# Placing every large SBUF tile of a decoder trunk at a multiple of 256 bytes

## The chip, the core and the metric

The kernel runs on one core of a Trainium2 chip. The metric is device time in microseconds (us), from runs of the whole kernel; lower is better. Engines are named as in the profile: PE is TensorE (PEld its weight loads), DVE is VectorE, ACT is ScalarE, POOL is GpSimd, SP is SyncE, whose queue (SPq) issues all the DMAs here.

## The reference

A decoder trunk of two layers on 1024 tokens of width 1024, 16 heads of 64. Each layer normalises, projects, mixes, gates and projects back:

```
h = rms_norm(x, norm_g[i])
if i % 2 == 0: o, gate = fox_mixer(h, ...)     # layer 1
else:          o, gate = dsw_mixer(h, cos, sin, ...)   # layer 2
x = x + (o * silu(gate)) @ w_out
```

The mixer of layer 1 ("fox") is causal attention over all earlier tokens with a forget bias: `s = q k / 8 + c_q - c_k`, softmax, times v, where `c` is a running sum of log-sigmoids and q and k are normalised per head. The mixer of layer 2 ("dsw") has three groups of queries, keys and values, with windows of 128 tokens at dilations 1, 4 and 16, rotary positions on the first 16 dimensions, and a softmax over the groups' log-sums that weighs their outputs.

## The kernel before

Matrices are held as pairs of fp16 numbers, a high part and the rest, so that each float32 product becomes three fp16 matmuls (`xh`·w high, `xh`·w low, `xl`·w high). A projection (L678, in `project`) takes one tile of 128 tokens against the 384 columns of a block of weights: 24 matmuls of 128 x 384, with a slice of `xh` or `xl` as the weights and the block's `w` as the moving operand. The output projections (L702, in `project_t`) do the reverse: `w` is loaded as weights and 512 columns of `xh` or `xl` move.

A block of weights goes through `raw` (loaded as float32, L605), a bound of its size (L615, L617), and the split into the fp16 pair `w` (L643, L644, or L646 to L648 on GpSimd). There are eight `raw` and eight `w` tiles of 3072 bytes a partition, two blocks' worth.

Attention runs by heads in pairs. `heads_tile` (L772 to L783) and `heads_pair` (L804 to L820) turn a projection into normalised queries and keys `hl`, a fp16 pair; a DMA transpose (L824) puts `hl` into `qk_t`, 12 blocks of 128 x 128. L844 makes the scores from `qk_t`, VectorE adds bias or mask and takes the minimum (L1091 in layer 1, L1319 in layer 2), ScalarE takes the exponential in place in `p` (L887; L1321, L1327) and casts it to the high half of `ph` (L890; L1331), GpSimd puts the rest into the low half (L893; L1332), and a second DMA transpose (L894; L1333) makes `ptt`, which is loaded as weights against the values `vt` (L901 to L903). In layer 2 the outputs of two groups go through HBM (`og` out, `cmb` back), are weighed on GpSimd (L1363, L1364), and are added to the third group's on VectorE (L1371).

The order of the work on every engine is set at the end by a planner (`order_engines`), which replays the recorded instructions with costs written into the program and fixes each engine's sequence. It knows tiles by name, shape and buffer count, and knows nothing of addresses.

SBUF tiles come from pools. `const`, `w`, `sb` and `sm` live through the kernel; a pool `layer` is opened for each layer, with a number of buffers for each tag. A pool puts its tiles one behind the other, each at the next multiple of 32 bytes of the partition. All pools are wrapped in the class `Listed`, which also notes each tile for the planner. Of the small tiles (statistics of 4 to 192 bytes a partition) there are many, and they shift what follows. Where the large tiles start, in bytes past a multiple of 256:

| tile | bytes a partition | before | after |
|---|---|---|---|
| `xh`, `xl` | 16384 | 128 | 0 |
| `raw`, `w`, `u`, `hl` | 2048 or 3072 | 96 | 0 |
| `p`, layer 1 / layer 2 | 512 to 4096 | 32 / 128 | 0 |
| `ph`, layer 1 / layer 2 | 1024 to 4096 | 32 / 224 | 0 |
| `ptt`, layer 1 / layer 2 | 1024 to 4096 | 32 / 224 | 0 |
| `qk_t` | 3072 | 128 | 0 |
| `vt` (three buffers) | 4128 | 32, 64, 96 | 0 |
| `og` (three buffers) | 1056 | 128, 160, 192 | 0 |
| `cmb` (four buffers) | 3168 | 224, 64, 160, 0 | 0 |

Of the kernel before, what the change touches and what calls it, by code (L numbers as in the profile page):

```python
# [84 lines left out]
            self.tick()  # L85


class Book:


# [16 lines left out]
class Listed:  # L107
# [2 lines left out]
        self.book, self.p, self.key, self.bufs, self.space = book, p, key, bufs, space  # L110

    def tile(self, shape, dtype, name, **kw):
        t = self.p.tile(shape, dtype, name=name, **kw)
        self.book.rows[t.tensor.name if hasattr(t, "tensor") else t.name] = (self.key + (kw.get("tag", name),), kw.get("bufs", self.bufs), self.space)
        return t
# [1419 lines left out]
```

## Time and profile before

| | us |
|---|---|
| median of 3 runs (lowest, highest) | 1687.83 (1684.5, 1690.51) |
| the profiled execution | 1688.37 |
| its span, first to last instruction | 1686.5 |
| idle time of PE in the span | 65.6 |

The page gives, for each engine, its busy time; the share of the chain that ended last ("PE pj L678 43%"); and, for groups of instructions, how often one ran, how long one took and what ended the idle time before it. Idle time of an engine that is not the bottleneck costs nothing. The DMA engines moved 292.84 MB in 662861 packets, 510208 of them under 512 bytes: the transposes move pieces of 256 bytes, 128 fp16 numbers.

The span has four parts: the start and the gates of layer 1 (to about 130 us), the attention of layer 1 (130 to 560), its output projection and the gates of layer 2 (560 to 740), and layer 2's attention (740 to 1640) with the last projection behind it.

### The profile page before, as it was taken

To read this page: it belongs to the slowest core of one execution; us is meant where nothing else is said; L and a number is where in the kernel's file an instruction comes from. 1 tells how busy PE (TensorE), PEld (TensorE's weight loads), DVE (VectorE), ACT (ScalarE), POOL (GpSimd) and SP (SyncE) were. 2 spreads that over 40 slices of the span, in tenths; PEclk is the share of its full clock that TensorE was granted. 3 is DMA by queue.
4 is the path that set the end of the run, shared out by engine and by line. 5 is a ranking of instruction groups with operands and counts; after the bars stand their busy time and mean duration, and the time that the engine had idled before them with its cause. 6 is when DMAs were issued, how large, how long until landed. Compare 5 with 4: busy or idle time off the path is not lost.

```text
span 1686.5 us, 37679 instructions
## 1 busy us (share of the span) xinstructions
PE 1620.9 (96%) x13342; PEld 1047.3 (62%) x13342; DVE 1184.2 (70%) x3663; ACT 1065.6 (63%) x2746; POOL 895.7 (53%) x1049
## 2 busy tenths in 40 slices
PE   6999999999988989999999999999999999999999
PEld 4666666666665436666666666666666666666644
DVE  7857677776777577567776787677776777767751
ACT  6656677676677456656666677566665666666630
POOL 5203566565545242145555566677686766757530
PEclk8999999999999999999999999999999999999999
DMA  7335999999999885347778798778787778878952
GB/s 250 110 122 127 199 213 205 203 185 207 213 195 215 230 264 174 126 91 150 148 150 164 158 214 186 151 151 191 170 165 151 151 174 160 186 150 170 218 157 100
DMA packets 662861, 292.84 MB, mean 174 GB/s; under 512 B 510208, under 2 KB 626944, under 8 KB 662672
## 3 DMA queue, kind: packets, MB, share of 16 engines
q1 hardware_dynamic: 662672, 290.44, 77.6%
q8 instruction: 104, 1.70, 0.4%
q14 instruction: 85, 0.70, 0.1%
HBM read 124.35 MB, written 41.22 MB: 98 GB/s over the span
## 4 chain that ended last, share of the span: by engine, by line
PE 57%; DMA 6%; DVE 6%; ACT 3%; issue 2%; SPq 1%; POOL 1%; DVEq 0%; ACTq 0%; POOLq 0%
PE pj L678 43%; PE pj L702 7%; PE s L844 4%; DMA ptt<-ph 3%; DMA qk_t<-hl 2%; DVE w L644 1%; PE ob L903 1%; PE ob L901 1%; PE ob L902 1%; DVE xs L1241 1%; SPq L894 1%; DMA yt<-y_d 1%; PE pt L712 0%; ACT w L643 0%; ACT ph L890 0%
## 5 line engine op out<-in xcount | busy, mean ns | idle before, releaser
L678 PE MATMUL pj<-w,xh 128*128 128x384 f16 (+2 forms) x4864 | 1174.9, 324 | 13.5 <-DVE w L644 5.9
L678 PE MATMUL pj<-w,xl 128*128 128x384 f16 (+2 forms) x2432 | 788.1, 324 | 5.5 <-DVE xl L1246 5.3
L678 PEld LDWEIGHTS <-xh 128*128 128x128 f16 x4864 | 466.8, 98 | 285.1 <-issue 7.2
L678 PEld LDWEIGHTS <-xl 128*128 128x128 f16 x2432 | 238.4, 98 | 163.5 <-issue 8.0
L893 POOL TENSOR_TENSOR ph<-p,ph 128x512 f16<-128x512 f32 (+3 forms) x176 | 172.7, 1003 | 154.0 <-issue 67.5
L819 POOL TENSOR_TENSOR hl<-u,hl 128x512 f16<-128x512 f32 x128 | 155.5, 1215 | 109.5 <-ACT hl L818 109.0
L1332 POOL TENSOR_TENSOR ph<-p,ph 128x768 f16<-128x768 f32 (+2 forms) x96 | 160.9, 1676 | 90.6 <-ACT ph L1331 80.0
L844 PE MATMUL s<-qk_t 128*128 128x128 f16 (+1 forms) x1504 | 163.7, 248 | 8.2 <-DMA qk_t<-hl 4.6
L702 PE MATMUL pj<-xh,w 128*128 128x512 f16 x512 | 158.2, 383 | 4.6 <-DVE xr L1471 2.9
L772 DVE TENSOR_TENSOR u<-pj,gr 128x256 f32<-128x256 f32 x256 | 107.5, 420 | 73.6 <-PE pj L678 72.2
L777 ACT ACTIVATE sq<-pj 128x256 f32<-128x256 f32 x256 | 96.5, 377 | 80.8 <-DVE u L772 80.1
L887 ACT ACTIVATE p<-p,acc 128x512 f32<-128x512 f32 (+2 forms) x192 | 111.4, 607 | 41.4 <-DVE acc L1091 39.9
L644 DVE SCALAR_TENSOR_TENSOR w<-raw,sws,w 128x768 f16<-128x768 f32 x96 | 127.0, 1324 | 10.2 <-ACT w L643 9.2
L844 PEld LDWEIGHTS <-qk_t 128*128 128x128 f16 x1504 | 115.5, 98 | 28.7 <-DMA qk_t<-hl 6.8
L702 PEld LDWEIGHTS <-w 128*128 128x128 f16 x768 | 74.5, 99 | 87.6 <-issue 8.4
L901 PEld LDWEIGHTS <-ptt 128*128 128x128 f16 x1136 | 106.0, 98 | 32.1 <-DMA ptt<-ph 21.9
L1321 ACT ACTIVATE p<-p,og 128x128 f32<-128x128 f32 (+1 forms) x256 | 104.2, 441 | 25.7 <-DVE og L1319 24.7
L615 ACT ACTIVATE jk<-raw 128x768 f16<-128x768 f32 (+2 forms) x88 | 72.2, 820 | 65.8 <-DMA raw<-in_w_dsw 38.1
L818 ACT CAST hl<-u 128x512 f16<-128x512 f32 x128 | 78.6, 614 | 55.0 <-DVE u L816 33.1
L783 DVE SCALAR_TENSOR_TENSOR vt<-pj,vt 128x128 f16<-128x128 f32 x256 | 73.5, 287 | 55.8 <-ACT vt L782 55.5
L902 PEld LDWEIGHTS <-ptt 128*128 128x128 f16 x1136 | 105.6, 97 | 10.0 <-issue 0.4
L903 PEld LDWEIGHTS <-ptt 128*128 128x128 f16 x1136 | 105.8, 97 | 0.5
(210 smaller groups left out, 2851.7 us busy)
## 6 DMA issues: line engine op xcount, KB each, us to landing
raw<-in_w_dsw SPq DMA_DIRECT2D x96, 384.0 KB, 4.0
raw<-in_w_fox SPq DMA_DIRECT2D x32, 384.0 KB, 4.0
og_d<-og SPq DMA_DIRECT2D x64, 132.0 KB, 3.0
cmb<-og_d SPq DMA_DIRECT2D x64, 132.0 KB, 2.8
bc<-c_d SPq DMA_DIRECT2D x32, 256.0 KB, 4.1
gs_d<-ge SPq DMA_DIRECT2D x32, 192.0 KB, 1.9
xt<-in_xt SPq DMA_DIRECT2D x16, 256.0 KB, 5.6
gsf<-gs_d SPq DMA_DIRECT2D x64, 64.0 KB, 2.9
```

Of the source, the lines that this page charges most:

```text
L644: nc.vector.scalar_tensor_tensor(w[:, 1, :, :n], raw, self.sw, w[:, 0, :, :n], ALU.mult, ALU.subtract)
L678: nc.tensor.matmul(ps[:, :n], a[:, k, cols], w.slab(k, j), start=(k == 0 and i == 0), stop=(k == KT - 1 and i == 2))
L702: nc.tensor.matmul(ps[m], w.slab(k, j)[:, m * P : (m + 1) * P], a[:, k, 512 * b : 512 * (b + 1)], start=(k == 0 and x == 0), stop=(k == KT ...
L772: nc.vector.tensor_mul(u[:, t % 2].rearrange("p (a b) d -> p a b d", a=2), ps[:, : 4 * HD].rearrange("p (a b d) -> p a b d", a=2, b=2), gr ...
L819: nc.gpsimd.tensor_sub(hl[:, :, :4, 1], u, hl[:, :, :4, 0])
L844: nc.tensor.matmul(s[:, c0 : c0 + cnt * P].rearrange("p (c s) -> p c s", c=cnt), qk[:, i, blk], kk[:, j : j + cnt, e], start=(h == 0), sto ...
L887: nc.scalar.activation(p, p, AF.Exp, bias=acc, scale=-1.0)
L893: (nc.gpsimd if pool_l else nc.vector).tensor_sub(ph[:, e, 1, cols], p, ph[:, e, 0, cols])
L901: nc.tensor.matmul(o[:, e, :], hi, vt[:, j, e, HD:], start=(b == 0), stop=False, skip_group_check=True)
L902: nc.tensor.matmul(o[:, e, :HD], hi, vt[:, j, e, :HD], start=False, stop=False, skip_group_check=True)
L903: nc.tensor.matmul(o[:, e, :], lo, vt[:, j, e, HD:], start=False, stop=(b == n - 1), skip_group_check=True)
L1332: nc.gpsimd.tensor_sub(ph[:, 1], st["p"], ph[:, 0])
```

## The change

Where a tile is made, `Listed.tile` now asks for a start at a multiple of 256 bytes if the tile is in SBUF and has 256 bytes or more a partition. PSUM and HBM tiles, and the small statistics, are left as they are.

```diff
+LINE = 256
+
+
 class Book:
...
     def tile(self, shape, dtype, name, **kw):
+        if self.space is None and np.prod(shape[1:]) * mybir.dt.size(dtype) >= LINE:
+            kw["align_bytes"] = LINE
         t = self.p.tile(shape, dtype, name=name, **kw)
         self.book.rows[t.tensor.name if hasattr(t, "tensor") else t.name] = (self.key + (kw.get("tag", name),), kw.get("bufs", self.bufs), self.space)
         return t
```

Tiles whose size is no multiple of 256 (`vt`, `og`, `cmb`) are padded up to the next; the others are only moved. The last tile ends at byte 228352 of a partition instead of 219232. No tile, shape, buffer count or instruction changes, and on all five engines the instructions stand in the same order and wait at the same places as before, so that there is no piece of an order to show. Views inside a tile keep their offsets: the slices of `cmb` at 1056 and 2112 bytes and those of `vt` at steps of 258 bytes do not start at a multiple of 256 afterwards either.

## The prediction

> **What bounds the kernel now.** I read the page first, then the stretches of the span, then TensorE's waits, and last the rows in which the same work is done on tiles that start at different places.
>
> ```profile
> span 1686.5 us, 37679 instructions
> PE 1620.9 (96%) x13342; PEld 1047.3 (62%) x13342; DVE 1184.2 (70%) x3663; ACT 1065.6 (63%) x2746; POOL 895.7 (53%) x1049
> ```
> TensorE (PE) is busy 96% of the span; nothing else passes 70%. Whatever a change gives to the other engines, it can give back at most the 1686.5 - 1620.9 = 65.6 us in which TensorE does not work, unless it makes a matmul itself shorter. The table of stretches says where those 65.6 us lie:
>
> ```profile
> core 0: us, PE busy (x) PEld busy (x) DVE busy (x) ACT busy (x) POOL busy (x), PEclk, DMA share, GB/s
> 0.00:40.00 40.00, 25.34 (x128) 17.42 (x128) 31.32 (x75) 27.12 (x59) 21.48 (x27) 0.87 0.74 261
> 130.00:560.00 430.00, 406.42 (x4143) 281.39 (x4140) 306.16 (x1003) 301.30 (x736) 234.62 (x227) 0.99 0.99 199
> 740.00:1640.00 900.00, 890.61 (x7283) 573.75 (x7281) 651.69 (x2139) 578.56 (x1635) 571.89 (x740) 1.00 0.79 167
> ```
> 40.00 - 25.34 = 14.7 us are the start. 430.00 - 406.42 = 23.6 us are the attention of layer 1, where the DMA engines are busy 0.99 of the time: this is the one stretch in which transfers are short. In the long stretch of layer 2 TensorE lacks 9.4 us of 900. What ended TensorE's idle times, over the whole span, as far as it bears on the change:
>
> ```profile
> PE o L901 <- DMA ptt<-ph: 11.2, 12, 2.1
> PE pj L678 <- DVE w L644: 5.9, 3, 2.6
> PE s L844 <- DMA qk_t<-hl: 4.6, 5, 2.3
> PE pt L712 <- DMA yt<-y_d: 4.2, 4, 2.5
> PE ob L901 <- DMA ptt<-ph: 1.6, 2, 1.2
> ```
> (Columns: total us, times, longest.) Waits for a transfer come to 11.2 + 4.6 + 4.2 + 1.6 = 21.6 us in 23 waits. Of these the DMA transposes hold 17.4 us in 19.
>
> **The change part by part.** No instruction is added, removed, resized or moved, and each engine waits at the same places for the same semaphores. What changes is where in a partition the big SBUF tiles start: before, hardly one starts at a multiple of 256 bytes (nearly all are 32, 96, 128, 160 or 224 bytes past one); afterwards all do. So the cost is that of the same instructions at other starts, and the rows of the kernel before already hold such comparisons, since equal work there runs on tiles that lie differently.
>
> TensorE. The projections of L678 stream `w`, which starts 96 past a multiple of 256; the output projections of L702 stream `xh` and `xl`, 128 past one.
>
> ```profile
> L678 PE MATMUL pj<-w,xh x4864: 269/326/528, 16.5 to 1585.4; 128*128 128x384 f16 x184, 128*128 128x256 f16 x6, 128*128 128x272 f16 x5
> L678 PE MATMUL pj<-w,xl x2432: 271/326/528, 18.8 to 1586.0; 128*128 128x384 f16 x178, 128*128 128x272 f16 x5, 128*128 128x256 f16 x5
> 1520.72 7.84 PE pj L678 x48
> 1529.77 7.80 PE pj L678 x48
> 1630.90 51.98 PE pj L702 x240
> 199.81 0.38 PE L844 MATMUL s<-qk_t 128*128 128x256 f16 x2
> 200.03 0.22 PE L1089 MATMUL s<-tri_b,ident_b 128*128 128x128 bf16 x1
> 200.09 0.38 PE L844 MATMUL s<-qk_t 128*128 128x256 f16 x2
> ```
> The first two count the matmuls of L678 (ns least/median/most), 7296 in all; the next three are rows of the chain (start, us, what), the last three of the timeline. 7.80 / 48 = 162.5 ns for 384 columns is 0.423 ns a column; 51.98 / 240 = 216.6 ns for 512 columns is 0.423 again. Two starts, 32 bytes apart in phase, give the same rate to the third digit. The score matmuls read both operands from `qk_t`, 128 past: two of them and the one behind begin at 199.81 and 200.03, 0.11 us for 256 columns, 0.43 ns a column at two digits. I take 0 for TensorE. Bounds: a matmul that costs one column more or less, 0.4 ns, in each of the 7296 of L678 is 3 us either way.
>
> ScalarE, VectorE, GpSimd. Three pairs:
>
> ```profile
> L887 ACT ACTIVATE p<-p,acc 128x256 f32<-128x256 f32 x32 | 15.2, 498 | 8.3 <-DVE acc L1091 8.3
> L1321 ACT ACTIVATE p<-p,og 128x256 f32<-128x256 f32 x112 | 53.0, 502 | 11.7 <-DVE og L1319 11.4
> L890 ACT CAST ph<-p 128x512 f16<-128x512 f32 x104 | 61.4, 609 | 11.1 <-DMA ptt<-ph 10.9
> L1331 ACT CAST ph<-p 128x512 f16<-128x512 f32 x32 | 19.7, 617 | 0.7
> L1371 DVE TENSOR_TENSOR ob<-ob,cmb x32: 424/437/438, 1092.9 to 1621.7; 128x260 f32<-128x260 f32 x32
> ```
> In layer 1 the scores `p` start 32 past, in layer 2 128 past: the same exponential in place takes 498 and 502 ns. The cast reads `p` and writes `ph`: 32 to 32 past in layer 1, 128 to 224 in layer 2, 609 and 617 ns. The VectorE row (ns least/median/most) is the best, because it holds an aligned case: the slice of `cmb` that L1371 reads lies 1056 bytes into a tile of 3168, and with four buffers it starts 0, 96, 192 and 32 past a multiple of 256. All 32 executions lie between 424 and 438 ns. So I take 0; the bound is that spread, 14 of 437 ns or 3%, with either sign. Even if every VectorE instruction gained it, TensorE's largest wait for VectorE, the 5.9 us on L644 above, would give 0.2 us.
>
> Transfers. Here the price is least known. Of a DMA transpose, the rows of one line hold issue and landing:
>
> ```profile
> L824 SPq DMA_TRANSPOSE qk_t<-hl x128: 1272/1466/3305, 136.7 to 1598.6; - x128
> DMA to landing us min/median/max: 3.6/4.3/6.2
> L894 SPq DMA_TRANSPOSE ptt<-ph x96: 1189/1796/4638, 149.4 to 554.8; - x96
> DMA to landing us min/median/max: 2.5/4.6/7.5
> L1333 SPq DMA_TRANSPOSE ptt<-ph x96: 1231/1442/3802, 746.0 to 1614.1; - x96
> DMA to landing us min/median/max: 3.0/4.3/7.3
> L894 SPq DMA_TRANSPOSE ptt<-ph x1: 1232/1232/1232, 154.7 to 154.7; - x1
> DMA to landing us min/median/max: 3.1/3.1/3.1
> ```
> The smallest of L894 moves 1024 bytes a partition, the smallest of L1333 2048, those of L824 all 3072. The undisturbed landings, 2.5, 3.0 and 3.6 us, grow evenly, 0.55 us for each 1024 bytes, although their sources start 32, 224 and 96 past a multiple of 256. The second tile of layer 1, at 154.7 us, moves 2048 bytes from 32 past and lands in 3.1 us, against 3.0 us from 224 past. So how far a piece reaches over a 256-byte line does not show. Whether reaching over it at all costs something does not show either, since no transpose of the kernel before is aligned. I take 0, by the pair 3.1 and 3.0, the nearest row; the ends are below.
>
> Sum: 1688.37 (the profiled execution's own time: 1686.5 of span and 1.9 around it) + 0 = 1688.4 us. The median of the three runs is 1687.83, their lowest 1684.5. I forecast 1687, a shade under both for the one term whose sign leans one way, the transposes.
>
> **The rivals.** *Transposes get shorter (faster).* A transposed piece of 256 bytes (128 fp16) now lies over two lines of 256 bytes, and afterwards in one. If each line touched were all that is paid, the slope would halve, 0.55 to 0.28 us for 1024 bytes, and a transpose of 3072 bytes would land 0.8 us earlier. In 19 waits of 17.4 us, 0.9 each and none below zero, some 13 us would go: 1675. The floor is all 21.6 us of TensorE's waits for transfers: 1667. What is late next is then the start and VectorE's 5.9 us on L644, which this leaves. For it speaks the DMA share of 0.99 in layer 1, where a shorter transfer also lets the next begin sooner; against it, nothing but that each piece pays the same whatever its overhang.
>
> *The same, graded.* If instead the bytes up to the next line were paid again, 32 of 288, 96 of 352 and 224 of 480 would be saved, or 1/9, 3/11 and 7/15. On 1.65 us (3 x 0.55) that is 0.2, 0.45 and 0.8 us for a transpose of L894, L824 and L1333; times the 12, 5 and 2 waits above, 2.2 + 2.3 + 1.6 = 6 us: 1682. But then 2048 bytes from 224 past would take 15/9 of the pieces' time from 32 past, 1.7 times, and the rows have 3.0 against 3.1 us. [...]
>
> *Equal starts collide (slower).* With every big tile on the same phase, engines that sweep tiles side by side could meet on the same lines of SBUF, where now `w`, `xh` and `ph` are staggered by 32 or more bytes. The place that decides is L678, which has no slack in layer 2 (890.61 of 900 us busy). One per cent on its 162.5 ns is 1.6 ns, times 7296 is 11.9 us: 1700. It decides from 0.4%, 5 us. Against it: the score matmuls read weights and moving columns from tiles of one phase, and keep the rate of the others.
>
> *Nothing can change because the change does not reach.* Slices of `cmb` (1056 bytes) and `vt` (258 bytes) start off the line afterwards too, so there the change does nothing. This gives 1688 and belongs to no change.
>
> **How the numbers follow.** Runs of this kernel differ by 6 us (1684.5 to 1690.5), so about 0.3%, 5 us, is what a measurement can tell. No change within 0.3%, from 1683 to 1693: 0.72. Transposes shorter: 0.17 (0.13 by lines touched, at 1675 and down to 1667; 0.04 graded, at 1682, since the landings contradict it). Collisions: 0.11, from 1693 to 1700. The range of 8 in 10 takes all of the first and the nearer half of the other two: 1676 to 1695.
>
> **What would show it.** Right: L678 at a median of 326 ns and 7.8 us for 48 in the chain; L887 and L1321 at 498 and 502, L1371 near 437 ns; least landings of the transposes still 2.5, 3.0 and 3.6 us; TensorE's waits for transfers near 21.6 us and layer 1 again near 406 of 430 us. The first rival would show in least landings of L1333 and L824 under 2.8 and 3.3 us and a DMA share under 0.95 in layer 1. The second would show in the 48 matmuls taking over 7.84 us. I would be wrong if a line of SBUF has a price that none of these offsets reveals, because all but `cmb`'s first slice were off it.

## The result, and the profile after

The change made the kernel faster: a median of 1672.25 us (1666.48 to 1676.36, five runs) against 1689.01 before (1684.5 to 1694.3), a ratio of 0.9898 with a 95% interval of 0.9866 to 0.9931, some 17 us or 1%. The forecast was 1687, no change, with a range of 1676 to 1695: the median lies below both. The profiled execution after is the slowest of the five, 1676.36 us with a span of 1674.5, so its profile shows 12 us of the 17.

The page's first lines, the transfers' line, and three rows of the chain, after (lines of the file stand five lower down than before: L678 is L683, L894 L899, L1333 L1338, L824 L829):

```profile
span 1674.5 us, 37679 instructions
PE 1622.5 (97%) x13342; PEld 1050.3 (63%) x13342; DVE 1182.2 (71%) x3663; ACT 1066.7 (64%) x2746; POOL 896.3 (54%) x1049
...
q1 hardware_dynamic: 662672, 290.44, 74.8%
```
```profile
1511.54 7.84 PE pj L683 x48
1529.38 7.80 PE pj L683 x48
1618.91 51.97 PE pj L707 x240
```
The engines do the same work: TensorE is busy 1622.5 us against 1620.9, the others within 2 us of before, and its matmuls keep their rates (7.80 us for 48, 51.97 for 240). TensorE's idle time is what fell, from 65.6 to 52.0 us. The DMA engines moved the same bytes in the same 662672 packets, but these took 74.8% of 1674.5 us instead of 77.6% of 1686.5: 1252.5 us against 1308.7, 56 us less on each of the 16 engines.

The groups that the prediction leaned on, after:

```profile
L892 ACT ACTIVATE p<-p,acc 128x256 f32<-128x256 f32 x32 | 15.2, 497 | 8.0 <-DVE acc L1096 7.3 <-POOL ph L898 0.7
L1326 ACT ACTIVATE p<-p,og 128x256 f32<-128x256 f32 x112 | 53.3, 503 | 12.6 <-DVE og L1324 12.2
L1376 DVE TENSOR_TENSOR ob<-ob,cmb x32: 424/437/438, 1079.6 to 1609.7; 128x260 f32<-128x260 f32 x32
```
The exponentials take 497 and 503 ns (498 and 502 before), the VectorE addition 424/437/438 as before. The transposes are another matter (issue in ns, landing in us, least/median/most):

```profile
L829 SPq DMA_TRANSPOSE qk_t<-hl x128: 1273/1424/3328, 136.3 to 1587.4; - x128
DMA to landing us min/median/max: 3.2/3.9/7.9
L899 SPq DMA_TRANSPOSE ptt<-ph x96: 1189/1671/5244, 149.1 to 540.1; - x96
DMA to landing us min/median/max: 2.4/4.3/8.0
L1338 SPq DMA_TRANSPOSE ptt<-ph x96: 1231/1408/4397, 732.7 to 1602.2; - x96
DMA to landing us min/median/max: 2.7/3.7/6.4
```
The least landings went from 2.5, 3.0 and 3.6 us to 2.4, 2.7 and 3.2 for 1024, 2048 and 3072 bytes a partition: 0.1 to 0.4 us, more the more bytes move. (The 0.1 at 1024 bytes is not clear of the spread: with `ph` aligned, the traces below have 2.3 to 2.5.)

Where the time went shows in the table of stretches, cut at the first score matmul and the last value matmul of each layer's attention; two rows before, then two after (columns as in the prediction):

```profile
146.40:561.10 414.70, 390.94 (x4066) 272.31 (x4063) 293.87 (x975) 293.03 (x709) 231.22 (x224) 0.99 1.00 202
756.90:1621.60 864.70, 857.25 (x7091) 555.40 (x7090) 631.13 (x2083) 562.74 (x1595) 559.83 (x726) 1.00 0.81 169
```
```profile
146.00:547.40 401.40, 388.17 (x4066) 273.78 (x4063) 293.22 (x974) 292.84 (x709) 231.58 (x224) 0.99 0.98 209
744.00:1609.60 865.60, 858.46 (x7092) 556.01 (x7091) 630.36 (x2083) 563.86 (x1594) 559.55 (x726) 1.00 0.77 168
```
Layer 1's attention is 13.3 us shorter, at least the whole of the 12 us that this profile gained. Its DMA share (the packets' time over 16 engines' time; it can pass 1, as a run below does with 1.07) stays at about one, 1.00 and 0.98: the same transfers go by faster, 209 GB/s against 202. Layer 2's attention, with shares of 0.81 and 0.77, takes as long as before although its transposes are quicker too. TensorE's waits for transfers, after:

```profile
PE o L906 <- DMA ptt<-ph: 7.3, 6, 2.9
PE pt L717 <- DMA yt<-y_d: 4.1, 2, 2.8
PE s L849 <- DMA qk_t<-hl: 3.2, 4, 1.4
PE ob L906 <- DMA ptt<-ph: 0.7, 1, 0.7
```
They fell from 21.6 us in 23 waits to 15.3 in 13.

### The profile page after: what moved, and what is told of

Same layout as the page of the kernel before. It is cut to its first block, busy times and chain, and to the rows that moved or that the text cites. A ratio compares the mean times of both kernels' runs of the same rounds, so it can differ in the third digit from the quotient of the medians.

```text
span 1674.5 us, 37679 instructions
## 1 busy us (share of the span) xinstructions
PE 1622.5 (97%) x13342; PEld 1050.3 (63%) x13342; DVE 1182.2 (71%) x3663; ACT 1066.7 (64%) x2746; POOL 896.3 (54%) x1049
## 2 busy tenths in 40 slices
DMA packets 662861, 292.84 MB, mean 175 GB/s; under 512 B 510208, under 2 KB 626944, under 8 KB 662672
## 3 DMA queue, kind: packets, MB, share of 16 engines
q1 hardware_dynamic: 662672, 290.44, 74.8%
## 4 chain that ended last, share of the span: by engine, by line
PE 81%; DVE 7%; DMA 5%; ACT 2%; issue 2%; SPq 1%; POOL 1%; DVEq 0%; ACTq 0%; POOLq 0%
PE pj L683 58%; PE pj L707 9%; PE s L849 7%; DMA ptt<-ph 2%; DVE w L649 2%; DMA qk_t<-hl 1%; PE o L906 1%; PE o L908 1%; PE ob L908 1%; PE ob L906 1%; PE o L907 1%; PE ob L907 1%; PE pt L717 1%; DMA yt<-y_d 1%; DVE xs L1246 0%
## 5 line engine op out<-in xcount | busy, mean ns | idle before, releaser
L683 PE MATMUL pj<-w,xh 128*128 128x384 f16 (+2 forms) x4864 | 1176.5, 325 | 12.0 <-DVE w L649 4.3
L683 PE MATMUL pj<-w,xl 128*128 128x384 f16 (+2 forms) x2432 | 789.1, 325 | 3.6 <-DVE xl L1251 3.6
L683 PEld LDWEIGHTS <-xh 128*128 128x128 f16 x4864 | 467.2, 98 | 286.2 <-issue 10.1
L683 PEld LDWEIGHTS <-xl 128*128 128x128 f16 x2432 | 238.5, 98 | 160.7 <-issue 7.6
L824 POOL TENSOR_TENSOR hl<-u,hl 128x512 f16<-128x512 f32 x128 | 155.5, 1215 | 114.1 <-ACT hl L823 109.4
L906 PEld LDWEIGHTS <-ptt 128*128 128x128 f16 x1136 | 106.2, 98 | 23.2 <-DMA ptt<-ph 12.3
```

The lines of the kernel that those rows point to most:

```text
L683: nc.tensor.matmul(ps[:, :n], a[:, k, cols], w.slab(k, j), start=(k == 0 and i == 0), stop=(k == KT - 1 and i == 2))
L824: nc.gpsimd.tensor_sub(hl[:, :, :4, 1], u, hl[:, :, :4, 0])
L906: nc.tensor.matmul(o[:, e, :], hi, vt[:, j, e, HD:], start=(b == 0), stop=False, skip_group_check=True)
```

## The experiments

In all but two of them (the ones on the planner's rate) the instructions stand in the order of the kernel before. The theory: a DMA transpose reads pieces of 256 bytes from SBUF, which cost more when they lie over two 256-byte lines; layer 1 is held by the sum of its transfers, so the saving counts there and nowhere else. Rivals: the writing side, plain transfers, the engines' own accesses; and, for layer 1, single waits rather than the sum.

**Only the transposes' tiles aligned.**

```diff
-        if self.space is None and np.prod(shape[1:]) * mybir.dt.size(dtype) >= LINE:
+        if self.space is None and kw.get('tag', name) in ('hl', 'ph', 'qk_t', 'ptt'):
```


> Only the tiles of the DMA transposes (sources hl and ph, destinations qk_t and ptt) start at a multiple of 256 bytes; every other tile starts where it falls. Theory A, the transposes' pieces of 256 bytes no longer lie over two lines: the whole gain is here, ratio 0.990, least landings 2.4, 2.7 and 3.2 us for 1024, 2048 and 3072 bytes a partition as in the changed kernel. Theory B, the gain comes from plain transfers or from the engines' own accesses: ratio 1.00 and least landings 2.5, 3.0 and 3.6 us.

Measured 1672.23 us, ratio 0.989 (0.9866 to 0.9914). The whole gain is in four tags of tiles, with least landings of 2.4, 2.7 and 3.2 us; `xh`, `xl`, `raw` and `w` lie where they lay before. A few other tiles have one of these tags too (`ptt` is also that of `xs`, `xsq` and `xrow`); the run with the destinations off, below, moves those of `ptt` and keeps the gain.

**All the other tiles aligned.**

```diff
-        if self.space is None and np.prod(shape[1:]) * mybir.dt.size(dtype) >= LINE:
+        if self.space is None and np.prod(shape[1:]) * mybir.dt.size(dtype) >= LINE and kw.get("tag", name) not in ("hl", "ph", "qk_t", "ptt"):
```


> Every large tile starts at a multiple of 256 bytes except hl, ph, qk_t and ptt, which start 64 to 128 bytes past one (ph of layer 1 at one or 96 past). Theory A: least landings of the transposes 2.5, 3.0 and 3.6 us where source and destination are off, ratio 0.998 to 1.002. Theory B, plain transfers or engine accesses: ratio 0.990 with the transposes as slow as before.

Measured 1688.96 us, 0.9991 (0.9973 to 1.0008): nothing. The expectation had the layers the wrong way round: it is layer 2 whose `ph` and `ptt` fell on a multiple of 256, while layer 1's `ph` lay 96 past and `hl` too. So the run tells more than was planned:

```profile
L829 SPq DMA_TRANSPOSE qk_t<-hl x128: 1273/1460/3267, 135.4 to 1605.4; - x128
DMA to landing us min/median/max: 3.6/4.1/7.5
L899 SPq DMA_TRANSPOSE ptt<-ph x96: 1195/1800/4633, 148.2 to 555.0; - x96
DMA to landing us min/median/max: 2.5/4.6/7.3
L1338 SPq DMA_TRANSPOSE ptt<-ph x96: 1231/1410/5202, 752.1 to 1620.1; - x96
DMA to landing us min/median/max: 2.7/3.7/7.2
```
Layer 2's `ptt` transposes are as quick as in the changed kernel (2.7), the others as slow as before (2.5, 3.6), and the kernel gains nothing. Quicker `ptt` transposes in layer 2 are worth nothing, and neither are the other tiles aligned here, `w`, `raw`, `xh`, `xl` and `p` among them.

**Reading side or writing side.** The four tags start at chosen places: the tile is made a little longer, and its data begin some bytes in. The edit is that of the run with the sources off; the other run has 0 for `hl` and `ph` and 32 for `qk_t` and `ptt`.

```diff
+LINE = 256
+STARTS = {'hl': 32, 'ph': 32, 'qk_t': 0, 'ptt': 0}
...
+        if self.space is None and tag in STARTS and True:
+            kw["align_bytes"] = LINE
+            pad = STARTS[tag] // mybir.dt.size(dtype)
...
+            t = self.p.tile([shape[0], pad + n], dtype, name=name, **kw)
...
+            t = t[:, pad:]
...
```


> As the run with the four aligned tiles, but the sources hl and ph start 32 bytes past a multiple of 256, the destinations at one. Theory A1, the line counts where the transpose reads: landings back at 2.5, 3.0 and 3.6 us, ratio 1.00. Theory A2, it counts where the transpose writes: 2.4, 2.7 and 3.2 us and ratio 0.990. Both sides count: between, near 2.9 and 3.4 us and 0.995.

> As the run with the four aligned tiles, but the destinations qk_t and ptt start 32 bytes past a multiple of 256, the sources at one. Theory A1, the reading side counts: 2.4, 2.7 and 3.2 us, ratio 0.990. Theory A2, the writing side counts: 2.5, 3.0 and 3.6 us, ratio 1.00.

Measured with the sources off: 1692.18 us, 1.0007 (0.9992 to 1.0023). With the destinations off: 1672.14 us, 0.9889 (0.9869 to 0.9908). Rows of layer 2's transpose, sources off, then destinations off:

```profile
L1352 SPq DMA_TRANSPOSE ptt<-ph x96: 1231/1448/4141, 745.9 to 1615.8; - x96
DMA to landing us min/median/max: 3.0/4.2/6.9
```
```profile
L1352 SPq DMA_TRANSPOSE ptt<-ph x96: 1231/1407/3879, 731.0 to 1600.5; - x96
DMA to landing us min/median/max: 2.7/3.7/7.7
```
The reading side is all of it; a destination 32 bytes past costs nothing that these runs can tell.

**Which line.** Sources 128 bytes past a multiple of 256 (`STARTS` of `hl` and `ph` 128, the others 0).

> Sources hl and ph start 128 bytes past a multiple of 256, destinations qk_t and ptt at one. If the line that counts is 256 bytes, each 256-byte piece lies over two lines as from 32 bytes past: least landings 2.45, 3.05 and 3.65 us and ratio 1.00. If the line is 128 or 64 bytes, a piece now touches as few lines as an aligned one: 2.4, 2.7 and 3.2 us and 0.989.

Measured 1689.96 us, 0.9987 (0.9974 to 1.0001).

```profile
L1352 SPq DMA_TRANSPOSE ptt<-ph x96: 1231/1445/3730, 749.0 to 1616.0; - x96
DMA to landing us min/median/max: 3.0/4.3/6.8
```
A start at 128 is worth as little as one at 32 (ratios of 0.9987 and 1.0007, a least landing of 3.0 us with both), so if lines are what counts, the line is not 128 bytes or less. That it is 256 bytes is not shown: a piece of 256 bytes that starts at a multiple of 256 lies within one line of 512 or 1024 bytes too.

What a single piece pays can be read from the packet records of transposes of 3072 bytes a partition that ran with no other packet over 64 bytes beside them. In the changed kernel (issued at 1105.99 us) each of the 1536 pieces takes at most 18 ns, and all are through in 1.54 us. In the kernel before (at 1119.22 us) they need 2.01 us: 327 pieces take 20 ns or more, up to 94, and the others at most 19. So not every piece that lies over a line is seen to pay; about one in five does, and why those is open.

**How the gain grows with what is aligned.** `STARTS` by layer: only `ph` of layer 1 at 0, or only `hl` (both layers) at 0; the other sources 32 past.

> Only ph of layer 1 starts at a multiple of 256; hl of both layers and ph of layer 2 start 32 bytes past one, destinations at one. Theory, the gain is DMA time saved in layer 1, where the DMA engines are busy 0.99: ph carries 36864 of the 49152 bytes a partition that are transposed per pair of heads there, three quarters, so three quarters of the 18 us: 13.5 us, ratio 0.992. Rival, what counts is the single wait of TensorE for a score transpose (qk_t): no more than half the gain, ratio 0.995 or above.

> Only hl starts at a multiple of 256 (both layers); ph starts 32 bytes past one, destinations at one. Theory of DMA time saved in layer 1: one quarter of the pieces there, 4.5 us, ratio 0.997. Rival (the waits for qk_t count): half the gain or more, 0.995 or below.

Measured: `ph` of layer 1 alone 1680.62 us, 0.9927 (0.9909 to 0.9945); `hl` alone 1686.42 us, 0.9965 (0.9953 to 0.9978). By the ratios that is 12.3 and 5.9 us, together 18.2, where all four tags gave 1.1%, 18.6; by the medians it is 10.8 and 5.0, together 15.8, against 18.1. By the pieces 13.5 and 4.5 were expected. Both rivals lie outside the intervals, if narrowly, and the gain goes roughly with the number of pieces in layer 1.

**More bytes into layer 1.** Four tags aligned; each `gsf` load brings 512 columns of the gate instead of 128, of which the same 128 are used. The planner's cost of that load is held at the old one.

```diff
+WIDE = 4
...
-                gs = st["gs"] = lay([P, P], F32, name="gsf", tag="gsl")
-                nc.sync.dma_start(gs, gs_d[t * P : (t + 1) * P, hp * P : (hp + 1) * P])
+                c0 = min(hp * P, D - WIDE * P)
+                gs = lay([P, WIDE * P], F32, name="gsf", tag="gsl")
+                nc.sync.dma_start(gs, gs_d[t * P : (t + 1) * P, c0 : c0 + WIDE * P])
+                st["gs"] = gs[:, hp * P - c0 : (hp + 1) * P - c0]
```


> The four tiles of the transposes aligned as in the changed kernel, but each of the 64 loads of the gate (gsf) in layer 1 brings four times the bytes (2048 a partition, of which 512 are used), 12.6 MB more in the same order of work; at the rate of the first 40 us (261 GB/s at a share of 0.74, so 353 at full) that is some 35 us of DMA time, more than alignment saves in layer 1 (0.99 of 415 us before, 0.96 of 401 after, 25 us). Theory, layer 1 is held by the total DMA time: the gain is gone, ratio 1.00 or above. Rival, each transpose's own latency counts and the queue has room: the gain stays, ratio 0.992 or below.

Measured 1700.2 us, 1.0058 (1.0035 to 1.008): 28 us over the same kernel without the bytes, so the gain is gone and more. The stretch of layer 1's attention without the bytes, then the stretch and TensorE's first wait with them:

```profile
146.70:546.30 399.60, 387.83 (x4066) 273.09 (x4063) 293.12 (x975) 292.33 (x709) 231.43 (x224) 0.99 0.99 210
```
```profile
147.20:573.20 426.00, 392.52 (x4066) 272.93 (x4063) 294.30 (x975) 293.93 (x709) 231.57 (x224) 0.99 1.07 227
```
```profile
PE o L907 <- DMA ptt<-ph: 20.8, 16, 3.1
```
No engine waits over 0.9 us for the loads of `gsf` or what reads them; the transposes behind them come late. In this order of the work layer 1 is held by the sum of its transfers: it takes 426.0 us with the bytes and 399.6 without.

**The planner told of quicker transposes.** The edit is that of the first run; the second has 220.

```diff
-        return 200.0 if "Transpose" in self.op else 300.0
+        return 280.0 if "Transpose" in self.op else 300.0
```


> The changed kernel with the planner's rate for a DMA transpose raised from 200 to 280 bytes a ns, as the aligned transposes need it (0.46 us for 131072 bytes); the order of the work on all engines is planned anew, so that steps behind a transpose are placed earlier. If layer 1 is held by how long its transfers take, an order that expects them sooner brings waits and not time: ratio 0.987 to 0.995. If it is held by where the planner put the steps: 0.985 or below.

> The changed kernel with the planner's rate for a transpose raised a little, from 200 to 220 bytes a ns; a new order on all engines. If the loss with 280 came from steps placed too early behind a transpose, a small step loses little or wins: ratio to the kernel before 0.985 to 0.992. If any new order loses what the old one had by tuning: 0.995 to 1.00.

Measured 1691.39 us with 280, 0.9997 (0.9986 to 1.0008), outside both expectations: the whole gain is lost. With 220, 1676.89 us, 0.9923 (0.9893 to 0.9952), between the two expectations and close to the first; it is not better than the changed kernel. The stretch of layer 1 and the first wait with 280:

```profile
146.40:566.30 419.90, 392.76 (x4066) 274.79 (x4064) 290.59 (x976) 292.48 (x710) 228.52 (x224) 0.98 0.96 200
```
```profile
PE o L906 <- DMA ptt<-ph: 19.9, 8, 4.8
```
Eight waits for `ptt` take 19.9 us here, against six of 7.3 in the changed kernel, though these transposes land as quickly (least and median 2.5 and 4.1 us, against 2.4 and 4.3). The DMA share is 0.96 of a longer stretch, so in this order the sum of the transfers does not account for the stretch alone. That fits steps placed by a landing that holds for an empty queue, but which of the moved steps does it was not taken apart, so this cause is argued and not shown. No version here beats the change as it is; aligning the four tags alone does the same with less room.

## Why the prediction was wrong

*The bound* was read rightly: TensorE, with 65.6 us that others could give back; the gain is 13.6 us of these. The prediction also named the stretch, layer 1 with its DMA share of 0.99, and then gave it no term in the sum.

*Nothing for TensorE, ScalarE, VectorE and GpSimd* held: rates and means stayed within 1%, and aligning all tiles but those of the four tags gave 0.9991.

*"I take 0, by the pair 3.1 and 3.0, the nearest row"*, for the transposes, is the step that failed: the runs with chosen starts show a cost where it had none, all of the 17 us. The pair compares two sources that both lie over the line, 32 and 224 past, so it could only tell whether the overhang's size matters. It was used as if it told whether lying over the line matters, which the prediction itself said no row could show. The bound was there, half the slope, 13 us and 1675, and it was put at 0.13. A term without a row that shows it should have been left between its ends.

*The size in the rival by lines touched.* It let the slope halve, 0.8 us for a transpose of 3072 bytes. Measured are 0.3 us at 2048 bytes and 0.4 at 3072: the landing grows by (3.2 - 2.4) / 2 = 0.40 us for 1024 bytes instead of 0.55. That is about half of the saving assumed, and yet the time came out at 1672, not 1675; that 1675 lies so near is luck, two errors against each other. The rival counted only what a named wait loses itself, and those waits fell by 21.6 - 15.3 = 6.3 us, half of the 12 in this profile. The rest fits a queue that is never empty, in which a transfer also gains from those ahead of it (argued, not taken apart): of some 414.7 x 1.00 - 401.4 x 0.98 = 21 us of DMA time saved in layer 1, the stretch got 13.3 shorter. The sign that the prediction gave for this rival came by half: the landings did fall under 2.8 and 3.3 us, but the DMA share from 130 to 560 us is 0.96 and not under 0.95, since the stretch gets shorter with its transfers.

*The graded rival* fell as argued: 32, 128 and 224 bytes past a multiple of 256 the least landing of 2048 bytes is 3.0 us, and 32, 96 and 128 past that of 3072 bytes is 3.6 or 3.7. From a multiple of 256 they are 2.7 and 3.2 us. All the other starts tried cost the same within 0.1 us, so the runs show a cost of not starting at a multiple of 256, and none that grows with how far past it the start lies.

*Collisions from equal starts* did not appear: 48 matmuls of L683 take 7.80 to 7.84 us as before.

## What to carry to other kernels

Try the SBUF sources of DMA transposes at a multiple of 256 bytes: for the four tags here it took 896 bytes more of a partition and gave a ratio of 0.989, and sources 128 past gave 0.9987. In this kernel it paid where the DMA share was about one (layer 1's attention, 1.00 and 0.98 before and after: 13.3 us, of which the waits that the profile names explain 6.3 at most); in layer 2's attention, with shares of 0.81 and 0.77, it paid nothing (864.7 us before, 865.6 after). When no row of a profile holds the case that a change makes, rows that are alike among themselves say nothing of it.

## What the runs showed of the hardware

For one plain store out of SBUF, too, the least landing was lower from a multiple of 256. That of `xn_d<-xg` (pieces of 512 bytes) is 2.9 us before, with `xg` 32 past, and 2.4 in the changed kernel and in the run with all the other tiles aligned, which both have `xg` at a multiple of 256; the medians are 3.5, 3.5 and 3.4. That of `xm_d<-xs` is 2.5 us before and in that run, with `xs` 32 and 128 past, and 2.4 in the changed kernel, with `xs` at a multiple of 256: 0.1 us, not clear of the spread. Rows of before, then of the run with all the other tiles aligned:

```profile
L1211 SPq DMA_DIRECT2D xn_d<-xg x16: 512/522/841, 542.5 to 633.9; - x16
DMA to landing us min/median/max: 2.9/3.5/5.1
L1247 SPq DMA_DIRECT2D xm_d<-xs x16: 512/558/678, 618.3 to 658.0; - x16
DMA to landing us min/median/max: 2.5/3.2/4.3
```
```profile
L1216 SPq DMA_DIRECT2D xn_d<-xg x16: 512/519/771, 542.1 to 638.2; - x16
DMA to landing us min/median/max: 2.4/3.4/5.8
L1252 SPq DMA_DIRECT2D xm_d<-xs x16: 512/558/682, 622.6 to 664.5; - x16
DMA to landing us min/median/max: 2.5/3.3/4.0
```
What it is worth in time no run tried by itself; in that run the whole came to nothing (0.9991).
